# A gated DeltaNet layer: the inverse of the chunks' matrices by fp32 products on whole operands instead of three fp16 products on halves

## The chip, the cores and the metric

One Trainium2 chip, of which the program uses one core. The metric is the device time of one execution in microseconds (us). Several executions were timed, and one more was recorded by the hardware profiler.

## The reference, cut to what matters

One layer with two kinds of heads over a prompt of 4096 rows, and one step for 8 sample rows. The prompt's four DeltaNet heads are computed in chunks: inside a chunk a unit lower triangular matrix of 64x64 is solved, and only then the state of 128x128 is carried on.

```python
lower = eye + beta[..., :, None] * jnp.einsum('nbhtd,nbhid->nbhti', k, k) * dec_strict
rhs = jnp.concatenate([(beta * jnp.exp(G))[..., None] * k, beta[..., None] * v], -1)
sol = lax.linalg.triangular_solve(lower, rhs, left_side=True, lower=True, unit_diagonal=True)
...
def step(s, xs):
    u = ut_c - jnp.einsum('bhcd,bhde->bhce', w_c, s)
    o = jnp.einsum('bhcd,bhde->bhce', qd_c, s) + jnp.einsum('bhti,bhie->bhte', aqk_c, u)
    s = gl_c[..., None, None] * s + jnp.einsum('bhcd,bhce->bhde', kd_c, u)
```

Everything is fp32. After the heads come a gate, sliding-window attention with 8 heads of its own, an output product with the 1024x1024 matrix and a LayerNorm.

## The kernel before, in words

The program has two phases. Phase 1 (to about 1135 us) runs over 16 superblocks `s` of 256 prompt rows, each of two chunks `c` of 128 rows with four heads; phase 2 does the attention, the gate and the output product and is not touched.

For a superblock, `front` makes keys, queries and values: 12 blocks of 128 columns, each by 24 fp16 products of 128x256 into the PSUM tile `pj` (weights `w`, rows `hT`, both as high and low fp16 halves), then a short convolution on VectorE (L315) and a SiLU (L321, L322; tiles `kqv`, `vv`). The products of keys with keys and queries go to `pga` (L41) and VectorE scales them to `U`, which is minus the strict lower part of the matrix, and `Aqk` (L379, L382).

The inverse of I - U is made in three levels. `lanes` writes the 32x32 diagonal blocks of all heads to DRAM and reads them back so that each partition holds one column problem, solves them on VectorE in 31 dependent pairs of operations (L421, L423; tiles `lt`, `LV`, `LU`), and brings the results back by DMA as the block diagonal `VTd`. `gdn_inv` then joins 32x32 blocks to 64x64 and 64x64 to 128x128 by four products per head: `px`, `pv`, `p2`, `p3` (PSUM tile `pgi`). In the kernel before, each of these products is three fp16 products (`mm3` with `P3`: high by high, high by low, low by high); the halves are made by `sub`, a copy to fp16 on ScalarE (L452) and a subtraction on VectorE (L453). The halves of `U` and `VTd` are made once per superblock (L384, L385; L434, L435).

`gdn_c` uses the inverse `V` of a chunk in fp32 products with the state (`pgi<-S,kqv`, `pgi<-r,V`, `pgi<-ut,Kd`, `pgi<-ut,Aqk`), and `S` goes on to the next chunk.

Beside this, phase 1 prepares the next superblock's rows (`xt`: `x`, `hT`, L253 to L256), weights for phase 2 (`prep`, `prep_s`: `stg`, `stt`, `wt`, L529 to L573) and the sample rows (`gate_cols`, `dec_a`: `xt`).

The code's order is not that of the engines. A scheduler at build time gives each engine a fixed sequence from a cost model of its own, so that the projections `pj<-hT,w` of the next superblock and the solve of `lanes` are laced into the inverse and `gdn_c` of this one. At run time each engine follows its sequence and waits on semaphores. The figures below call two parts of a superblock's period by their first PE instruction: **part A** from the first `pgi<-S,kqv` (start of `gdn_c`) to the first `pga<-kqv` of the next superblock, and **part B** from there to the next `pgi<-S,kqv`; part B has the `pga` products and the inverse.

Of the kernel before, what the change touches and what calls it, by code (L numbers as in the profile page):

```python
# [33 lines left out]
def body(ctx, tc, I, O, seq):  # L34
# [5 lines left out]
    def mm(out, l, r, st=True, sp_=True):  # L40
        pe.matmul(out, l, r, start=st, stop=sp_)  # L41
# [69 lines left out]
    with ExitStack() as p1:  # L111
# [124 lines left out]
        XE = w1p.tile([128, 2, 4, 128], F16, name="XE")  # L236
        XZ = w1p.tile([128, 2, 4, 128], F16, name="XZ")
        V64 = w1p.tile([128, 2, 4, 64], F16, name="V64")
        VR = w1p.tile([128, 2, 4, 64], F16, name="VR")
        for t in (VTd, XE, XZ, V64, VR):  # L240
            pool.memset(t, 0.0)
# [18 lines left out]
        def front(s, hT, ahead):  # L260
# [26 lines left out]
            U = wk.tile([128, 8, 128], F32, name="U", bufs=1)  # L287
            U16 = wk.tile([128, 2, 8, 128], F16, name="U16", bufs=1)
# [94 lines left out]
            vt, vt16 = lanes(s, U)  # L383
            act.activation(U16[:, 0], U, AF.Copy)  # L384
            dve.tensor_sub(U16[:, 1], U, U16[:, 0])  # L385
# [17 lines left out]
            return kqv, G, sc, U16, Aqk, Kd, Vn, eGl, vt, vt16  # L403

        def lanes(s, U):

            d1, d2 = D1[s % 2], D2[s % 2]
            d1v = d1.rearrange("(m b) (i t) -> b i m t", b=4, t=32)
            for b in range(4):
                bs = slice(32 * b, 32 * b + 32)  # L410
                sp.dma_start(d1v[b], U[bs, :, bs])
            LU = w1p.tile([128, 32, 32], F32, name="LU", bufs=1)
            for c in range(4):
                sp.dma_start(LU[32 * c:32 * c + 32].rearrange("p a b -> p (a b)"), d1)
            LV = w1p.tile([128, 8, 32], F32, name="LV", bufs=1)
            dve.tensor_copy(LV.rearrange("p a b -> p (a b)"), lv0)
            lt = w1p.tile([128, 8, 32], F32, name="lt", bufs=1)
            for j in range(31, 0, -1):
                j0 = j // 4
                n = 8 - j0  # L420
                dve.tensor_mul(lt[:, j0:, 0:j], LV[:, j0:, j:j + 1].to_broadcast([128, n, j]),  # L421
                               LU[:, None, 0:j, j].to_broadcast([128, n, j]))
                dve.tensor_add(LV[:, j0:, 0:j], LV[:, j0:, 0:j], lt[:, j0:, 0:j])  # L423
            d2w = d2.rearrange("l (j c i) -> c l j i", c=4, i=32)
            for c in range(4):
                sp.dma_start(d2w[c], LV[32 * c:32 * c + 32])
            d2r = d2.rearrange("(m b) (q i) -> b q m i", b=4, i=32)
            vt = VTd
            for b in range(4):
                bs = slice(32 * b, 32 * b + 32)  # L430
                sp.dma_start(vt[bs, :, bs], d2r[b])
            vt16 = w1p.tile([128, 2, 8, 2, 32], F16, name="vt16")
            ve = vt.rearrange("p m (a b) -> p m a b", b=64)[:, :, :, 0:32]
            act.activation(vt16[:, 0], ve, AF.Copy)  # L434
            dve.tensor_sub(vt16[:, 1], ve, vt16[:, 0])  # L435
            return vt, vt16

        P3 = ((0, 0), (0, 1), (1, 0))

        def gdn_inv(c, U16, vt, vt16):  # L440

            V = wk.tile([128, 4, 128], F32, name="V", bufs=2)
            Vo = wk.tile([128, 2, 4, 2, 32], F16, name="Vo", bufs=1)
            xe, xz, v64, vr = XE, XZ, V64, VR
            m0 = 4 * c

            def mm3(out, l, r):
                for n, (a, b) in enumerate(P3):
                    mm(out, l(a), r(b), n == 0, n == 2)

            def sub(dst, src):
                act.activation(dst[0], src, AF.Copy)  # L452
                dve.tensor_sub(dst[1], src, dst[0])  # L453
# [5 lines left out]
            vo = V.rearrange("p h (a b) -> p h a b", b=64)[:, :, :, 32:64]  # L459
            sub([Vo[:, 0], Vo[:, 1]], vo)  # L460
            px = pgi.tile([128, 4, 2, 32], F32, name="pgi")
            for h in range(4):
                mm3(px[:, h], lambda a: U16[:, a, m0 + h, :], lambda b: vt16[:, b, m0 + h])
            sub([xe[:, z].rearrange("p h (a b) -> p h a b", b=64)[:, :, :, 0:32] for z in range(2)], px)
            pv = pgi.tile([128, 4, 2, 32], F32, name="pgi")
            for h in range(4):
                mm3(pv[:, h], lambda a: xe[:, a, h, :], lambda b: Vo[:, b, h])
            dve.tensor_copy(V[0:32, :, 32:64], pv[0:32, :, 0, :])
            dve.tensor_copy(V[64:96, :, 96:128], pv[64:96, :, 1, :])
            sub([vr[64:128, z] for z in range(2)], V[64:128, :, 64:128])  # L470
# [3 lines left out]
            sub([v64[0:64, z] for z in range(2)], pt[0:64, :, 0:64])  # L474
            p2 = pgi.tile([128, 4, 64], F32, name="pgi")
            for h in range(4):
                mm3(p2[:, h], lambda a: U16[:, a, m0 + h, :], lambda b: v64[:, b, h, :])
            sub([xz[64:128, z, :, 0:64] for z in range(2)], p2[64:128])
            p3 = pgi.tile([128, 4, 64], F32, name="pgi")
            for h in range(4):  # L480
                mm3(p3[:, h], lambda a: xz[:, a, h, :], lambda b: vr[:, b, h, :])
# [227 lines left out]
        def ahead(s):  # L709
            if s < NS:  # L710
                nxt[0] = xt(s, load_x(s))

        for s in range(NS):
            kqv, G, sc, U16, Aqk, Kd, Vn, eGl, vt, vt16 = front(s, nxt[0], lambda: ahead(s + 1))
            Vs = [gdn_inv(c, U16, vt, vt16) for c in range(2)]
# [741 lines left out]
```

## Time and profile before

| | us |
|---|---|
| median of 3 executions (2236.66 to 2239.43) | 2238.08 |
| the profiled execution | 2235.32 |
| its span, first to last instruction | 2233.5 |
| TensorE matmul busy (PE) | 2098.6 (94%) |
| VectorE busy (DVE) | 1831.9 (82%) |
| ScalarE busy (ACT) | 1269.1 (57%) |

Read it so: PE is the TensorE's matmul stream, PEld its weight loads, which run beside it; the granted clock is that of the TensorE as a share of 2.4 GHz, 0.982 over the span. Busy times are unions of the instructions' times; matmuls in a burst overlap, so the burst is much shorter than their number times the time of one.

### The profile page before, as it was taken

How to read it: one execution, taken by the hardware profiler on the slowest of the kernel's cores; microseconds unless marked ns; L12 is line 12 of the kernel's file. 1: busy time of each engine (PE TensorE's matmuls, PEld its weight loads, DVE VectorE, ACT ScalarE, POOL GpSimd, SP SyncE). 2: the span in 40 equal slices, each digit the busy share in tenths (PEclk: the TensorE clock that was granted, in tenths of full speed). 3: DMA queues.
4: the chain of work that ended last, by engine and by line, in shares of the span. 5: the costliest groups of instructions: out<-in, count | busy, mean ns of one | idle time of the engine just before them, and what ended most of it. 6: DMA issues, size and time to landing. Idle time of an engine off the chain costs nothing.

```text
span 2233.5 us, 48900 instructions
## 1 busy us (share of the span) xinstructions
PE 2098.6 (94%) x18287; PEld 1497.6 (67%) x18287; DVE 1831.9 (82%) x5546; ACT 1269.1 (57%) x3601; POOL 163.4 (7%) x284
## 2 busy tenths in 40 slices
PE   6989999999989999898999999999999999999997
PEld 4877888878778888777676777776445545444443
DVE  7778889888889989888878977776786787888877
ACT  6666877666767776655446666666443333334332
POOL 1101111111111111011000000000000000000000
PEclk9999999999999999999999999999998999999999
DMA  8333332332233332213153111110532333323222
GB/s 331 105 114 92 130 91 93 119 105 68 88 98 107 107 115 81 67 51 114 54 215 119 59 60 60 61 58 23 222 100 91 131 114 114 117 87 132 95 98 72
DMA packets 141679, 232.21 MB, mean 104 GB/s; under 512 B 62852, under 2 KB 75448, under 8 KB 135272
## 3 DMA queue, kind: packets, MB, share of 16 engines
q1 hardware_dynamic: 140144, 228.53, 30.1%
q8 instruction: 144, 2.36, 0.4%
q14 instruction: 95, 0.78, 0.1%
q10 hardware_dynamic: 1296, 0.55, 0.1%
HBM read 154.07 MB, written 76.09 MB: 103 GB/s over the span
## 4 chain that ended last, share of the span: by engine, by line
PE 53%; DVE 28%; ACT 11%; DMA 4%; issue 3%; POOL 0%; POOLq 0%; SPq 0%; ACTq 0%; DVEq 0%
PE pp L1042 21%; PE pj L41 11%; PE pgi L41 6%; DVE kqv L315 5%; DVE lt L421 3%; PE pga L41 3%; ACT Sm L872 3%; DVE LV L423 3%; PE po L41 2%; PE tr L41 2%; PE tr L889 2%; DMA x<-in_xT_dram 1%; DVE kqv L322 1%; PE xt L41 1%; PE pS L41 1%
## 5 line engine op out<-in xcount | busy, mean ns | idle before, releaser
L41 PE MATMUL pj<-hT,w 128*128 128x256 f16 x4608 | 575.7, 275 | 3.4 <-ACT hT L255 2.6
L41 PEld LDWEIGHTS <-w 128*128 128x128 f16 x4800 | 450.0, 99 | 65.1 <-issue 11.4
L1042 PEld LDWEIGHTS <-S 128*128 128x128 f16 x1536 | 150.6, 99 | 171.4 <-issue 5.0
L41 PEld LDWEIGHTS <-hT 128*128 128x128 f16 x2048 | 159.8, 98 | 68.8 <-issue 4.1
L41 PE MATMUL pj<-wq,hT 128*128 128x512 f16 x768 | 194.8, 379 | 1.1 <-DVE qt L783 0.6
L315 DVE SCALAR_TENSOR_TENSOR kqv<-u,cols,kqv 128x256 f32<-128x256 f32 x384 | 181.9, 480 | 3.7 <-ACT kqv L313 3.1
L1042 PE MATMUL pp<-wz,S 128*128 128x512 f16 x768 | 182.1, 383 | 0.0
L1042 PE MATMUL pp<-wo,S 128*128 128x512 f16 x768 | 171.3, 379 | 0.7 <-DVE zs L1218 0.6
L872 ACT ACTIVATE Sm<-Sm,nm 128x256 f32<-128x256 f32 (+1 forms) x256 | 125.5, 492 | 56.0 <-DVE nm L869 56.0
L1042 PE MATMUL pp<-wz,hT 128*128 128x512 f16 x576 | 131.9, 380 | 1.2 <-ACT zs L1129 1.2
L421 DVE TENSOR_TENSOR lt<-LV,LU 128x60 f32<-128x60 f32 (+24 forms) x496 | 120.2, 242 | 5.8
L1042 PE MATMUL pp<-wo,A 128*128 128x512 f16 x540 | 122.1, 379 | 0.0
L865 DVE CUSTOM_DVE_ANT_0 Sm<-pS,swam 128x256 f32<-128x256 f32 (+1 forms) x256 | 96.2, 415 | 28.2 <-PE tr L889 27.3
L423 DVE TENSOR_TENSOR LV<-LV,lt 128x60 f32<-128x60 f32 (+24 forms) x496 | 103.4, 208 | 5.8
L1042 PEld LDWEIGHTS <-hT 128*128 128x128 f16 x612 | 59.8, 98 | 71.8 <-issue 2.8
L41 PE MATMUL pj<-wkv,hT 128*128 128x256 f16 x768 | 105.6, 273 | 0.0
L1081 POOL TENSOR_TENSOR rs<-rs,cf 128x1 f32<-128x1 f32 (+1 forms) x33 | 22.8, 692 | 1070.7 <-DVE rs L1080 1070.7
L41 PE MATMUL pga<-kqv 128*128 128x256 f32 x256 | 72.2, 401 | 24.2 <-DVE kqv L322 24.1
L1042 PEld LDWEIGHTS <-A 128*128 128x128 f16 x540 | 52.8, 99 | 62.0
L1023 ACT ACTIVATE S<-zt 128x512 f16<-128x512 f32 x64 | 40.3, 630 | 85.7 <-DVE zt L1029 81.4
L1136 ACT ACTIVATE zs<-zs 128x512 f32<-128x512 f32 x48 | 30.2, 629 | 101.3 <-DVE zs L1135 101.2
L315 DVE SCALAR_TENSOR_TENSOR vv<-u,cols,vv 128x256 f32<-128x256 f32 x192 | 82.3, 479 | 1.7 <-ACT vv L313 1.0
(378 smaller groups left out, 4574.7 us busy)
## 6 DMA issues: line engine op xcount, KB each, us to landing
hT<-hD SPq DMA_DIRECT2D x32, 1024.0 KB
x<-in_xT_dram SPq DMA_DIRECT2D x32, 512.0 KB
hD<-hT SPq DMA_DIRECT2D x16, 1024.0 KB
x<-in_x_prompt_dram SPq DMA_DIRECT2D x60, 256.0 KB
out_y_prompt_dram<-x SPq DMA_DIRECT2D x60, 256.0 KB
stg<-in_ws_dram SPq DMA_DIRECT2D x16, 512.0 KB
LU<-D SPq DMA_DIRECT2D x64, 128.0 KB
wS<-wt SPq DMA_DIRECT2D x16, 512.0 KB
```

The source lines that it names most:

```text
L41: pe.matmul(out, l, r, start=st, stop=sp_)
L315: dve.scalar_tensor_tensor(d, u[:, b2, j:j + 256], cwj(j, blk), d, op0=ALU.mult, op1=ALU.add)
L322: dve.scalar_tensor_tensor(dst, th, 1.0, dst, op0=ALU.add, op1=ALU.mult)
L421: dve.tensor_mul(lt[:, j0:, 0:j], LV[:, j0:, j:j + 1].to_broadcast([128, n, j]), LU[:, None, 0:j, j].to_broadcast([128, n, j]))
L423: dve.tensor_add(LV[:, j0:, 0:j], LV[:, j0:, 0:j], lt[:, j0:, 0:j])
L865: dve.tensor_tensor_reduce(Sm[:, h, k0:256], pS[:, h2, k0:256], swam[:, k0:256], 0.125, -1e30, op0=ALU.add, op1=ALU.max, accum_out=mx[:, h ...
L872: act.activation(Sm[:, h, k0:256], Sm[:, h, k0:256], AF.Exp, bias=nm[:, h:h + 1], accum_out=sm_[:, h:h + 1])
L889: pe.transpose(pt[:, h2, kb, :], Sm[:, h + h2, kb * 128:(kb + 1) * 128], ident)
L1023: act.activation(q[:, 0], src, AF.Copy)
L1042: pe.matmul(dst.rearrange("p (u c) -> p u c", c=128), A[:, hi, k, :], W[:, k // 2::2, q, wi, k % 2, :], start=new and n == 0, stop=n == 11 ...
L1081: pool.tensor_tensor(rs[0:n, 1:2], rs[0:n, 0:1], half_neg[0:n, 0:1], op=ALU.pow)
L1136: act.activation(zs, zs, AF.Silu, scale=IWS)
```

## The change

The four products take whole fp32 operands: one fp32 product per head and level in place of three fp16 products. The halves, the tiles for them and the operations that make them are gone; `U` gets a second buffer, since the products now read it directly; `VTd` and `V` are read in place. DMAs and all other products stay as many as they were.

```diff
-        XE = w1p.tile([128, 2, 4, 128], F16, name="XE")
-        XZ = w1p.tile([128, 2, 4, 128], F16, name="XZ")
-        V64 = w1p.tile([128, 2, 4, 64], F16, name="V64")
-        VR = w1p.tile([128, 2, 4, 64], F16, name="VR")
+        XE = w1p.tile([128, 4, 128], F32, name="XE")
+        XZ = w1p.tile([128, 4, 128], F32, name="XZ")
+        V64 = w1p.tile([64, 4, 64], F32, name="V64")
...
-            U = wk.tile([128, 8, 128], F32, name="U", bufs=1)
-            U16 = wk.tile([128, 2, 8, 128], F16, name="U16", bufs=1)
+            U = wk.tile([128, 8, 128], F32, name="U", bufs=2)
...
-            vt, vt16 = lanes(s, U)
-            act.activation(U16[:, 0], U, AF.Copy)
-            dve.tensor_sub(U16[:, 1], U, U16[:, 0])
+            vt = lanes(s, U)
...
-            vt16 = w1p.tile([128, 2, 8, 2, 32], F16, name="vt16")
-            ve = vt.rearrange("p m (a b) -> p m a b", b=64)[:, :, :, 0:32]
-            act.activation(vt16[:, 0], ve, AF.Copy)
-            dve.tensor_sub(vt16[:, 1], ve, vt16[:, 0])
-            return vt, vt16
+            return vt
...
-            def mm3(out, l, r):
-                for n, (a, b) in enumerate(P3):
-                    mm(out, l(a), r(b), n == 0, n == 2)
-
-            def sub(dst, src):
-                act.activation(dst[0], src, AF.Copy)
-                dve.tensor_sub(dst[1], src, dst[0])
...
-            vo = V.rearrange("p h (a b) -> p h a b", b=64)[:, :, :, 32:64]
-            sub([Vo[:, 0], Vo[:, 1]], vo)
+            ve, vo = quarters(vt[:, m0:m0 + 4])[:, :, :, 0:32], quarters(V)[:, :, :, 32:64]
             px = pgi.tile([128, 4, 2, 32], F32, name="pgi")
             for h in range(4):
-                mm3(px[:, h], lambda a: U16[:, a, m0 + h, :], lambda b: vt16[:, b, m0 + h])
-            sub([xe[:, z].rearrange("p h (a b) -> p h a b", b=64)[:, :, :, 0:32] for z in range(2)], px)
+                mm(px[:, h], U[:, m0 + h, :], ve[:, h])
+            act.activation(quarters(XE)[:, :, :, 0:32], px, AF.Copy)
             pv = pgi.tile([128, 4, 2, 32], F32, name="pgi")
             for h in range(4):
-                mm3(pv[:, h], lambda a: xe[:, a, h, :], lambda b: Vo[:, b, h])
+                mm(pv[:, h], XE[:, h, :], vo[:, h])
             dve.tensor_copy(V[0:32, :, 32:64], pv[0:32, :, 0, :])
             dve.tensor_copy(V[64:96, :, 96:128], pv[64:96, :, 1, :])
-            sub([vr[64:128, z] for z in range(2)], V[64:128, :, 64:128])
...
-            sub([v64[0:64, z] for z in range(2)], pt[0:64, :, 0:64])
+            act.activation(V64, pt[0:64, :, 0:64], AF.Copy)
             p2 = pgi.tile([128, 4, 64], F32, name="pgi")
             for h in range(4):
-                mm3(p2[:, h], lambda a: U16[:, a, m0 + h, :], lambda b: v64[:, b, h, :])
-            sub([xz[64:128, z, :, 0:64] for z in range(2)], p2[64:128])
+                mm(p2[:, h], U[0:64, m0 + h, :], V64[:, h, :])
+            act.activation(XZ[64:128, :, 0:64], p2[64:128], AF.Copy)
             p3 = pgi.tile([128, 4, 64], F32, name="pgi")
             for h in range(4):
-                mm3(p3[:, h], lambda a: xz[:, a, h, :], lambda b: vr[:, b, h, :])
+                mm(p3[:, h], XZ[64:128, h, :], V[64:128, h, 64:128])
```

The scheduler then orders all engines anew. On TensorE, in the inverse of superblock 8 in the middle of phase 1, a piece around the second product (`pgi<-Vo,XE`) stands so before; `w_5_360` is a projection's weight, and each fp16 product has a weight load (LDWEIGHTS) of its own in the list:

```order
L41 LDWEIGHTS w_5_360
L41 MATMUL pj<-hT,w_5_360 128x256
L41 LDWEIGHTS XE
L41 MATMUL pgi<-Vo,XE 128x64
L41 LDWEIGHTS w_5_360
L41 MATMUL pj<-hT,w_5_360 128x256
```

The same place in the change; an fp32 product is one row here, its weight loads not being listed apart, and x4 are the four heads:

```order
L440 MATMUL pgi<-cf,VTd 128x128 x4
L41 MATMUL pgi<-VTd,U 128x64 x4
L41 MATMUL pga<-kqv 128x256
L41 LDWEIGHTS w_10_398
L41 MATMUL pj<-hT,w_10_398 128x256
L41 MATMUL pgi<-V,XE 128x64 x4
```

What moved: the inverse now begins among the `pga` products of the next superblock, and fewer projections stand in it. Over superblocks 1 to 12 the sequence before has on average 197 projections in part A and 89 in part B; in the change they are 236 and 50.

On VectorE, the inverse of superblock 8 before, from the low half of `vt` on:

```order
L435 TENSOR_TENSOR vt_9323<-VTd,vt_9323 128x512
L315 SCALAR_TENSOR_TENSOR vv<-u,cols,vv 128x256 x4
L453 TENSOR_TENSOR Vo<-V,Vo 128x256
L453 TENSOR_TENSOR XE<-pgi,XE 128x8x32
L668 TENSOR_TENSOR dt_10702<-xt,deg 128x4
L256 TENSOR_TENSOR hT<-x,hT 128x512
L468 COPY V<-pgi 32x4x32
L469 COPY V<-pgi 32x4x32
L322 SCALAR_TENSOR_TENSOR vv<-th,vv 128x1024
```

And in the change, from the first chunk's inverse (the copies to `V`, L450 and L451) through the second's, and on into `gdn_c` (`r`, `ut`):

```order
L450 COPY V<-pgi 32x4x32
L451 COPY V<-pgi 32x4x32
L380 TENSOR_TENSOR Aqk<-pga,dec 128x256
L649 TENSOR_TENSOR dt_9839<-xt,deg 128x4
L650 SCALAR_TENSOR_TENSOR ddl<-dy,dt_9839 128x4
L651 TENSOR_TENSOR ddl<-ddl,dbe 128x4
L652 TENSOR_TENSOR dt_9839<-xt,deg 128x4
L653 TENSOR_TENSOR doT<-ddl,dqk 128x4
L654 TENSOR_TENSOR doT<-doT,dt_9839 128x4
L313 SCALAR_TENSOR_TENSOR vv<-u,cols,vv 128x256 x2
L474 SCALAR_TENSOR_TENSOR r<-pgi,G,Vn 128x128 x4
L313 SCALAR_TENSOR_TENSOR vv<-u,cols,vv 128x256 x2
```

What moved: of the subtractions nothing is left, and work that stood among them (the last convolutions and the SiLU of `vv`, the low halves of `hT`, the preparation of phase 2's weights) now stands behind `r`, that is in part A.

## Rows read from the trace of the kernel before

**Rows 1.** The page: busy time of the engines, the span in 40 slices.

```profile
PE 2098.6 (94%) x18287; PEld 1497.6 (67%) x18287; DVE 1831.9 (82%) x5546; ACT 1269.1 (57%) x3601; POOL 163.4 (7%) x284
PE   6989999999989999898999999999999999999997
PEclk9999999999999999999999999999998999999999
```

**Rows 2.** Windows: superblock 0, superblocks 1 to 13, superblock 14; bounds at `pgi<-cf,VTd`.

```profile
core 0: us, PE busy (x) PEld busy (x) DVE busy (x) ACT busy (x) POOL busy (x), PEclk, DMA share, GB/s
158.50:220.70 62.20, 54.02 (x474) 46.68 (x472) 52.35 (x170) 37.71 (x121) 9.60 (x12) 0.90 0.31 99
220.70:1047.50 826.80, 772.90 (x7753) 668.73 (x7752) 728.47 (x2546) 566.85 (x1833) 108.90 (x194) 0.99 0.30 95
1047.50:1102.20 54.70, 45.90 (x382) 33.82 (x381) 45.96 (x168) 26.69 (x81) 1.20 (x2) 0.91 0.27 83
```

**Rows 3.** Waits of PE, 220.7 to 1047.5 us: total, times, longest.

```profile
PE pga L41 <- DVE kqv L322: 19.7, 13, 2.1
PE tr L41 <- DVE g L283: 8.2, 7, 2.8
PE pgi L41 <- ACT V L452: 3.3, 7, 1.8
...
PE tr L355 <- DVE kqv L322: 3.2, 4, 1.0
```

**Rows 4.** Windows over part A of superblocks 1 to 12: one, and the sum.

```profile
684.81:722.27 37.46, 34.87 (x324) 30.81 (x325) 36.49 (x139) 27.45 (x91) 7.16 (x11) 1.00 0.30 100
...
sum 462.90, PE 427.14 PEld 382.05 DVE 436.46 ACT 325.81 POOL 88.25; mean PE 35.59 PEld 31.84 DVE 36.37 ACT 27.15 POOL 7.35
```

**Rows 5.** Windows over part B of the same superblocks: one, and the sum.

```profile
722.27:749.18 26.91, 25.95 (x290) 21.76 (x290) 23.42 (x73) 18.74 (x56) 0.82 (x4) 1.00 0.33 93
...
sum 297.90, PE 283.70 PEld 233.89 DVE 239.84 ACT 200.07 POOL 13.89; mean PE 23.64 PEld 19.49 DVE 19.99 ACT 16.67 POOL 1.16
```

**Rows 6.** Timeline of PE and PEld: start, length, shape and number of a burst.

```profile
678.73 0.51 PE L41 MATMUL pgi<-vt,U 128*128 128x64 f16 x12
691.05 1.06 PE L41 MATMUL pgi<-ut,Aqk 128*128 128x128 f32 x8
699.45 4.86 PE L41 MATMUL pj<-hT,w 128*128 128x256 f16 x43
729.80 0.95 PE L41 MATMUL xt<-dkq,stg 128*128 128x2 f32 x8
729.69 0.97 PEld L41 LDWEIGHTS xt<-dkq,stg 128*128 128x128 f32 x8
```

**Rows 7.** Instruction groups with mean times, PE and PEld, all of phase 1.

```profile
L41 PE MATMUL pgi<-vt,U x384: 189/193/261, 159.4 to 1110.9; 128*128 128x64 f16 x192
L41 PE MATMUL pgi<-ut,Aqk x256: 275/275/275, 180.4 to 1129.7; 128*128 128x128 f32 x128
L41 PEld LDWEIGHTS pgi<-ut,Aqk x256: 192/192/192, 180.3 to 1129.6; 128*128 128x128 f32 x128
```

**Rows 8.** Groups on VectorE by form, 220.7 to 1047.5 us: busy, mean ns, idle before.

```profile
L322 DVE SCALAR_TENSOR_TENSOR vv<-th,vv 128x1024 f32<-128x1024 f32 x13 | 15.9, 1221 | 0.9 <-ACT th L321 0.7
L385 DVE TENSOR_TENSOR U<-U,U 128x1024 f16<-128x1024 f32 x13 | 15.9, 1220 | 1.3 <-ACT U L384 1.3
L453 DVE TENSOR_TENSOR XZ<-pgi,XZ 64x256 f16<-64x256 f32 x26 | 11.1, 428 | 4.6 <-ACT XZ L452 3.9
L453 DVE TENSOR_TENSOR Vo<-V,Vo 128x256 f16<-128x256 f32 x26 | 11.0, 422 | 5.6 <-ACT Vo L452 5.4
L256 DVE TENSOR_TENSOR hT<-x,hT 128x512 f16<-128x512 f32 x48 | 32.4, 683 | 0.1
L435 DVE TENSOR_TENSOR vt<-VTd,vt 128x512 f16<-128x512 f32 x13 | 9.0, 689 | 3.4 <-ACT vt L434 3.4
L559 DVE TENSOR_TENSOR wt<-stg,wt 128x1024 f16<-128x1024 f32 x12 | 14.6, 1221 | 0.0
```

**Rows 9.** The same on ScalarE.

```profile
L384 ACT ACTIVATE U<-U 128x1024 f16<-128x1024 f32 x13 | 13.7, 1057 | 0.3
L452 ACT ACTIVATE Vo<-V 128x256 f16<-128x256 f32 x26 | 10.7, 412 | 0.3
```

More of the change, by code (lines that the diff above doesn't have):

```diff
@@ L235, in body @@
         VTd = w1p.tile([128, 8, 128], F32, name="VTd")
-        XE = w1p.tile([128, 2, 4, 128], F16, name="XE")
-        XZ = w1p.tile([128, 2, 4, 128], F16, name="XZ")
-        V64 = w1p.tile([128, 2, 4, 64], F16, name="V64")
-        VR = w1p.tile([128, 2, 4, 64], F16, name="VR")
-        for t in (VTd, XE, XZ, V64, VR):
+        XE = w1p.tile([128, 4, 128], F32, name="XE")
+        XZ = w1p.tile([128, 4, 128], F32, name="XZ")
+        V64 = w1p.tile([64, 4, 64], F32, name="V64")
+        for t in (VTd, XE, XZ):
             pool.memset(t, 0.0)
@@ L402, in front @@
                     act.activation(Vn[:, m, :], pv[:, h, :], AF.Copy, scale=sc[:, 0, m:m + 1])
-            return kqv, G, sc, U16, Aqk, Kd, Vn, eGl, vt, vt16
+            return kqv, G, sc, U, Aqk, Kd, Vn, eGl, vt
         def lanes(s, U):
@@ L431, in lanes, with gdn_inv, quarters @@
                 sp.dma_start(vt[bs, :, bs], d2r[b])
-            vt16 = w1p.tile([128, 2, 8, 2, 32], F16, name="vt16")
-            ve = vt.rearrange("p m (a b) -> p m a b", b=64)[:, :, :, 0:32]
-            act.activation(vt16[:, 0], ve, AF.Copy)
-            dve.tensor_sub(vt16[:, 1], ve, vt16[:, 0])
-            return vt, vt16
-        P3 = ((0, 0), (0, 1), (1, 0))
-        def gdn_inv(c, U16, vt, vt16):
+            return vt
+        def gdn_inv(c, U, vt):
             V = wk.tile([128, 4, 128], F32, name="V", bufs=2)
-            Vo = wk.tile([128, 2, 4, 2, 32], F16, name="Vo", bufs=1)
-            xe, xz, v64, vr = XE, XZ, V64, VR
             m0 = 4 * c
-            def mm3(out, l, r):
-                for n, (a, b) in enumerate(P3):
-                    mm(out, l(a), r(b), n == 0, n == 2)
-            def sub(dst, src):
-                act.activation(dst[0], src, AF.Copy)
-                dve.tensor_sub(dst[1], src, dst[0])
+            def quarters(t):
+                return t.rearrange("p h (a b) -> p h a b", b=64)
             pb = pgi.tile([128, 4, 128], F32, name="pgi")
@@ L713, in body @@
         for s in range(NS):
-            kqv, G, sc, U16, Aqk, Kd, Vn, eGl, vt, vt16 = front(s, nxt[0], lambda: ahead(s + 1))
-            Vs = [gdn_inv(c, U16, vt, vt16) for c in range(2)]
+            kqv, G, sc, U, Aqk, Kd, Vn, eGl, vt = front(s, nxt[0], lambda: ahead(s + 1))
+            Vs = [gdn_inv(c, U, vt) for c in range(2)]
             for c in range(2):
```

## The prediction

> **What bounds the kernel now.** I read the page first: TensorE (PE) is busy 94% of the span and VectorE (DVE) 82%, and the slices show PE near full from one end to the other, the granted clock being 0.99 in the middle of phase 1 [rows 1, 2]. So nothing on PE is free unless it falls into one of PE's few idle spots. Then I cut phase 1 into windows. In superblocks 1 to 13 PE is busy 772.9 of 826.8 us, so 53.9 us are idle, 4.1 per superblock of 63.6; superblocks 0 and 14 have 8.2 and 8.8 us idle each, since there are no projections to lace in at either end [rows 2]. The list of PE's waits says whom the idle time belongs to: 31.1 of the 53.9 us are waits for VectorE, before the `pga` products (19.7), for the decay `g` (8.2) and before the transposes of the keys (3.2); the largest wait on ScalarE is 3.3 [rows 3].
>
> VectorE is not late everywhere. Cut into the two parts, superblocks 1 to 12 take 38.6 us in part A (462.9/12) with PE busy 35.6 and DVE 36.4, and 24.8 us in part B (297.9/12) with PE 23.6 and DVE 20.0 [rows 4, 5]. Part A is thus VectorE's: 94% busy, it ends when VectorE gives up the last `kqv`, and PE waits there. Part B, with the inverse, is PE's: 95% busy, while DVE stands at 81% and itself waits for ScalarE's halves [rows 5, 8]. Over both, PE and DVE hand the bound to each other once per superblock.
>
> **The change, part by part.**
>
> *Products on PE.* A group (one product for four heads) is now twelve fp16 matmuls of 64 columns. Such a burst lasts 0.51 us with 0.193 for one, so a matmul costs (0.51-0.193)/11 = 0.029, a group 0.35 us [rows 6, 7]. An fp32 product appears in the trace as two matmuls with two weight loads: the `gdn_c` products are 32 chunks of four, and 256 of each are counted [rows 7]. With 128 columns a pass costs (1.06-0.275)/7 = 0.112. No fp32 product of 64 columns with 128 columns of weights is there, so its price is bounded. From above: with only 2 columns the eight weight loads of four products still take 0.97 us, (0.97-0.192)/7 = 0.111 each [rows 6]; narrower columns buy nothing, the weight load paces it. Eight of these are 0.89 us. From below: if only columns counted and fp32 were four times a 64-column matmul, sixteen by 0.029, 0.46 us. I take 0.89, because 64 columns lie between the 2 and the 128 that cost the same. So a group costs 0.54 us more; eight groups per superblock 4.3, all sixteen 69 us, superblocks 1 to 13 alone 56.
>
> The Trainium skill ("FP8 and Floating Point Precision", TensorE Precision Notes) says that true fp32 is four passes through the array. By that rule alone, four against three, a group would cost 0.12 more and the whole kernel some 15 us of PE, an estimate from that page. The rows disagree as far as narrow operands go: two records per product, each held at 0.111 by its weights.
>
> 56 us more on 772.9 are 829 us, more than the 826.8 that these superblocks now take. Even if PE never waited again, the middle of phase 1 would be 2 us longer. This is the main argument: VectorE's relief can only fill PE's idle time, which the products have already used up.
>
> *Work taken from VectorE and ScalarE.* Per superblock: the low halves of `U` (1.22 us) and `VTd` (0.69), and ten subtractions of about 0.42 (five for each chunk; two of the five rows stand for all): 6.1 us of DVE busy time, and about 1.2 us of waits for ScalarE in front of those that are shown ((1.3+4.6+5.6+3.4)/13) [rows 8]. ScalarE loses the copies of `U` (1.06), `VTd` and, twice, of `Vo` and `VR` (0.41 each) [rows 9]; it is 57% busy, and I cost that at nothing. Were all in VectorE's part, it would be worth its whole time. But only `U`'s low half lies in part A, by the order in five of twelve superblocks; the rest lies in part B, where PE is the bound.
>
> *The chain of a chunk's inverse.* Before, a product waits for the high half, then PE does one matmul and the low half (0.42) comes behind it. Now there is one copy and then 0.89 us. Four times (0.42 + 0.35) against four times 0.89: nearly even, so in superblock 0, where nothing covers the chain, I cost the change at nothing.
>
> *What the new order moves.* Projections in part A rise from 197 to 236 per superblock and fall from 89 to 50 in part B. A projection costs 4.86/43 = 0.11 us [rows 6], so 4.3 us of PE go from B to A. Six fp32 transposes of `vv` (0.11 each) and eighteen small products of the decay (0.03 each, the smallest spacing shown) go with them: 1.1. Behind `r`, thus in part A, VectorE now has 2.6 more low halves of `hT` (0.68 each, 1.8), the SiLU of `vv` and one convolution more (1.22+0.48), some 2.3 us of the preparation for phase 2 (most of it `wt` at 1.22), less 0.5 for `U`: together +5.3 (durations from [rows 8], numbers of instructions counted in the two orders).
>
> *Sum.* Part A: PE 35.6+4.3+1.1 = 41.0, with 0.5 for ScalarE's waits 41.5; DVE 36.4+5.3 = 41.7, with the 2.2 us for which it stands idle there now 43.9. The two engines are almost level, so I take a value between, 42.8, or 4.2 more than now. Part B: PE 23.6-4.3-1.1+4.3 = 22.5, and with its present 1.2 of waits 23.7, 1.1 less. Together +3.1 per superblock, 40 us for thirteen. At the ends: superblock 0 nothing; superblock 14 has in the new order 27 projections in its inverse where it had none, against 8.8 us idle, for which I give back 4; superblock 15 lies under phase 2's work on a full PE and pays most of its 4.3, say 3. That is +39 on the profiled execution's 2235.3, or **2274 us**. The median of the runs is 2238.1, 0.1% above that execution; I leave this as it is.
>
> What is late next: in part A VectorE again, now with more to do and less of PE's idle time to hide it; in part B the copies on ScalarE between two groups.
>
> **The rivals.**
>
> *The weight loads hide (the other side).* If a group cost its columns only, 0.46, part B would be 23.7-3.4 = 20.3, and the new order, which has moved 5.4 us of PE into part A, would be repaid: 41.5 to 42.8 + 20.3 = 61.8 to 63.1 against 63.4, thus 2210 to 2230. It decides at about 0.5 us per group. For it speaks that weight loads run beside matmuls; against it that four products of two columns, between projections, take their full 0.95 us [rows 6]. The page on four passes, named above, would lead here.
>
> *PE alone is the bound.* If VectorE's relief removes its waits outright, part A is 41.5 and part B, without the waits for low halves, 23.0: 64.5, +1.1 per superblock, 2250. For it: DVE loses 6.1 us of 56 (728.47/13) [rows 2]. Against it: it gains 5.3 of work in the very part where it was late.
>
> *VectorE sets part A and part B gains nothing.* 43.9 + 24.8 = 68.7, +5.3, 2304. For it: fewer projections lie between two dependent groups, so PE may stand while ScalarE copies (0.4 us each, eight per superblock). Against: four to eight projections or a `pga` product are still put into nearly every such place.
>
> **How the numbers follow.** Forecast, 2260 to 2292: 0.53. PE alone, 2244 to 2260: 0.20. VectorE in part A and waits in B, above 2292: 0.16. Weight loads hide: 0.11, of which I give 0.07 to faster and 0.04 to the same. What this kernel's measurement can tell from no change is about 0.2%, 4.5 us. Faster 0.07, same 0.05 (with 0.01 from the lower edge of PE alone), slower 0.88. The range reaches from PE alone to the third rival's value: 2249 to 2303.
>
> **What the profile after would show.** Right: 64 fp32 records in place of 96 fp16 ones per superblock for the four products; bursts of eight at about 0.111 us a pass; the rows L452 and L453 for halves gone; PE busy up by 65 to 70 us, DVE down by some 85 to 95; superblocks 1 to 13 some 40 us longer, part A about 43 us with DVE still near 95%, part B about a microsecond shorter, phase 2 as it was. Wrong in the price, if the bursts of 64 columns show 0.06 or 0.2 a pass. Wrong in the order, if the waits of PE for `kqv` and `g` are gone (then 2250) or if long waits for ScalarE appear before `pgi<-V,XE`, `pgi<-V,U` or `pgi<-V,XZ` (then 2300).

## The result, and the profile after

The change takes 2310.93 us (median of 4 executions, 2309.41 to 2316.99) against 2238.76 for the kernel before beside it: ratio 1.0335, 95% interval 1.0318 to 1.0352. It is slower, as forecast, but by 72 us and not by 36: 2310.9 lies above 2274 and above the range's upper end of 2303. One execution of e5 below (2480.36 us) ran at a granted clock of 0.83 and is left out of the comparisons.

The page of the profiled execution (2309.41 us, span 2307.6), the lines of [rows 1]:

```profile
PE 2174.7 (94%) x17775; PEld 1580.8 (69%) x17775; DVE 1743.9 (76%) x5354; ACT 1218.8 (53%) x3505; POOL 172.0 (7%) x282
PE   6989999999999999999898999999999999999997
PEclk9988999999999999999999999999999999999999
```

TensorE (PE) has 76 us more and 512 records less (32 for each superblock), VectorE (DVE) 88 us less. PE's share is 94% as before: its idle time has hardly shrunk (132.9 us, was 134.9). In the clock, slices 3 and 4 (115 to 231 us, superblock 0) have become an 8. Over the span the clock is 0.975, was 0.982: what is missing to full clock is some 58 us against 40, an estimate from these shares of the two spans. So up to 18 of the 76 us are a slower clock and not more work.

The windows of [rows 2], bounds again at `pgi<-cf,VTd`:

```profile
157.89:227.79 69.90, 62.45 (x444) 55.26 (x442) 46.95 (x159) 34.89 (x115) 9.72 (x12) 0.83 0.27 89
227.79:1105.31 877.52, 827.07 (x7292) 731.24 (x7291) 654.96 (x2380) 525.61 (x1748) 118.06 (x194) 0.98 0.28 88
1105.31:1169.21 63.90, 57.86 (x440) 43.94 (x438) 46.13 (x177) 27.41 (x89) 2.21 (x3) 1.00 0.30 97
```

The span grew by 74.1 us: superblock 0 by 7.7 (forecast 0), superblocks 1 to 13 by 50.7 (forecast 40), superblock 14 by 9.2 (forecast -4), and the rest by 7.1 (forecast 3; 2307.6 - 1169.2 against 2233.5 - 1102.2); the start is 0.6 shorter. In superblocks 1 to 13 PE is busy 54.2 us more and idle 50.4 us, was 53.9.

PE's timeline in the inverse of superblock 8, against [rows 6]:

```profile
704.29 1.00 PE L41 MATMUL pgi<-VTd,U 128*128 128x64 f32 x8
705.77 1.10 PE L41 MATMUL pgi<-V,XE 128*128 128x64 f32 x8
709.20 1.10 PE L41 MATMUL pgi<-V,U 64*128 64x64 f32 x8
710.77 1.10 PE L41 MATMUL pgi<-V,XZ 64*128 64x64 f32 x8
```

Eight passes a group, from 1.00 to 1.10 us with the last one's own 0.27 to 0.30 in it: some 0.11 a pass, and with that the 0.89 of the forecast.

PE's waits in superblocks 1 to 13, against [rows 3]:

```profile
PE pga L41 <- DVE kqv L320: 19.8, 13, 2.2
PE tr L41 <- DVE g L282: 12.1, 9, 2.6
PE tr L353 <- ACT G L332: 3.8, 3, 1.9
```

VectorE has a tenth less to do there (655 us, was 728), and PE waits for `kqv` as long as before (19.7) and for `g` longer (8.2). Long waits for ScalarE's copies before `pgi<-V,XE`, `pgi<-V,U` or `pgi<-V,XZ` have not come up.

Part A and then part B of superblocks 1 to 12, the sums, against [rows 4, 5]:

```profile
sum 540.76, PE 498.92 PEld 450.93 DVE 485.77 ACT 377.69 POOL 103.86; mean PE 41.58 PEld 37.58 DVE 40.48 ACT 31.47 POOL 8.65
...
sum 275.31, PE 270.06 PEld 228.80 DVE 124.84 ACT 111.82 POOL 7.50; mean PE 22.50 PEld 19.07 DVE 10.40 ACT 9.32 POOL 0.63
```

Part A takes 45.1 us (forecast 42.8), part B 22.9 (23.7): 68.0 for a superblock, 4.6 more than before and 0.3 more than the price of the products alone. (What lies outside these twelve superblocks in the middle is 4.6 us shorter than before, so that the thirteen grew by 50.7.) VectorE's relief is real, but it shows as idle time of VectorE in part B (10.4 busy of 22.9).

The clock differs in these windows too: eleven of the 24 show 0.93 to 0.96 in the change, three before. One of part A and one of part B:

```profile
584.03:633.01 48.98, 45.27 (x424) 41.22 (x424) 42.92 (x163) 35.04 (x112) 8.67 (x13) 0.95 0.41 135
351.80:377.67 25.87, 25.77 (x192) 22.27 (x192) 11.96 (x36) 11.26 (x33) 0.57 (x3) 0.93 0.21 52
```

Length times what is missing to 1.00, added up, gives some 19 us in the change and 5 before, an estimate: about 14 of the 54 us that PE is busy longer. What makes the clock fall in these places is not shown.

### The profile page after: what moved, and what is told of

Its sections match the earlier page's. It is cut to its first block, busy times and chain, and to the rows that moved or that the text cites. A ratio compares the mean times of both kernels' runs of the same rounds, so it can differ in the third digit from the quotient of the medians.

```text
span 2307.6 us, 47590 instructions
## 1 busy us (share of the span) xinstructions
PE 2174.7 (94%) x17775; PEld 1580.8 (69%) x17775; DVE 1743.9 (76%) x5354; ACT 1218.8 (53%) x3505; POOL 172.0 (7%) x282
## 4 chain that ended last, share of the span: by engine, by line
PE 47%; DVE 14%; ACT 6%; issue 2%; DMA 2%; POOL 0%; POOLq 0%; SPq 0%; ACTq 0%; DVEq 0%
PE pp L1023 20%; PE pj L41 10%; PE pgi L41 6%; DVE kqv L313 2%; ACT Sm L853 2%; PE po L41 2%; PE tr L870 2%; DVE lt L417 1%; PE pga L41 1%; PE pS L41 1%; PE tr L41 1%; DVE LV L419 1%; DMA dw<-in_wdec_dram 1%; DVE bst L1058 1%; DVE x L1066 1%
## 5 line engine op out<-in xcount | busy, mean ns | idle before, releaser
L41 PE MATMUL pj<-hT,w 128*128 128x256 f16 x4608 | 566.8, 275 | 3.2 <-ACT hT L254 2.6
L41 PEld LDWEIGHTS <-w 128*128 128x128 f16 x4800 | 456.6, 99 | 58.1 <-issue 3.6
L853 ACT ACTIVATE Sm<-Sm,nm 128x256 f32<-128x256 f32 (+1 forms) x256 | 125.5, 492 | 88.7 <-DVE nm L850 88.6
L377 DVE SCALAR_TENSOR_TENSOR U<-pga,sc,dec 128x128 f32<-128x128 f32 x128 | 39.1, 345 | 66.2 <-PE pga L41 65.9
```

The costliest lines, as they stand in the source:

```text
L377: dve.scalar_tensor_tensor(U[:, m, :], pa[:, h2, 1, :], sc[:, 3, m:m + 1], decs[c][:, 2 * hp + h2, :], op0=ALU.mult, op1=ALU.mult)
L853: act.activation(Sm[:, h, k0:256], Sm[:, h, k0:256], AF.Exp, bias=nm[:, h:h + 1], accum_out=sm_[:, h:h + 1])
```

## The experiments

*Theory 1*: the time follows TensorE's own work, and VectorE's relief is worth nothing. Rivals: *theory 2*, the new order lengthens part A; *theory 3*, the relief is worth something and a larger price hides it. Times are medians; the ratios are to the kernel before in the same series.

**The relief alone, and the price alone.** Two kernels made from the one before. In the first (e1):

```diff
-            dve.tensor_sub(U16[:, 1], U, U16[:, 0])
-            dve.tensor_sub(vt16[:, 1], ve, vt16[:, 0])
-                dve.tensor_sub(dst[1], src, dst[0])
-                for n, (a, b) in enumerate(P3):
-                    mm(out, l(a), r(b), n == 0, n == 2)
+                for _ in P3:
+                    mm(out, l(0), r(0))
```

> The kernel before without any of the subtractions that make the low halves (U, VTd and the ten of a superblock), TensorE's work unchanged: each of the four products issues three fp16 matmuls on the high halves, of which the last stands (so the products are fp16 products of the high halves alone). VectorE loses its 88 us, TensorE gains nothing. Its order at build time already is that of the change: 233 projections in part A and 51 in part B per superblock (before 197 and 89, change 236 and 50). Theory 1 (time is TensorE's, the relief is worth nothing): 2234 to 2242, waits for kqv and g as before. Theory 2 (the new order, by itself, lengthens part A, because VectorE's work piles up behind r): 2245 to 2265, part A 41 to 43 us. Theory 3 (the relief is worth VectorE's waits, but the change hides it under a larger price on TensorE): 2205 to 2225, waits for kqv and g well under 20 us.

Measured: 2230.17, ratio 0.9971 (0.9957 to 0.9984), 6 us. Superblocks 1 to 13:

```profile
218.53:1026.38 807.85, 753.99 (x7701) 666.00 (x7700) 655.41 (x2380) 561.57 (x1822) 104.97 (x194) 0.99 0.30 95
1026.38:1088.42 62.04, 54.17 (x477) 39.84 (x476) 46.05 (x178) 31.31 (x100) 2.32 (x3) 1.00 0.31 105
```

The second row is superblock 14. The middle is 19 us shorter, but superblock 14 is 7.3 longer and the rest behind it 4.4: with the new order, work that stood in the middle comes later. That answers theory 2 too: this order, with 233 projections in part A, costs nothing as a whole. In all, 88 us of VectorE are worth 6, and not by filled waits: PE is idle 53.9 us in the middle as before (807.85 - 753.99), and over the span 142.0, was 134.9. What fell is its busy time, with as many records (18287) in another order. Theory 3 falls, theory 1 was off by the 6.

In the second (e2), VectorE keeps its work and PE gets more:

```diff
+                for _ in range(4 + h % 2):
+                    mm(out, l(0), r(0))
                 for n, (a, b) in enumerate(P3):
```

> The kernel before with all halves, and 18 more fp16 matmuls of 64 columns in each group (four or five more per head, overwritten by the three that count), so that a group takes 30 times 0.029 = 0.87 us, the price of the fp32 group, while VectorE keeps its subtractions. Its order has 236 projections in part A and 51 in part B. Theory 1: before plus 128 times 0.52 = 67 us, that is 2300 to 2310, hardly less than the change. Theory 2: the same order with more work on VectorE, so part A is longer than in the change: 2320 to 2340. Theory 3: the relief is missing, so that the time is the change plus what the relief is worth, 2325 or more.

Measured: 2308.67, ratio 1.0322 (1.0294 to 1.0350), +72 for 67 us of matmuls. That is the change's time without fp32 and without the relief, though not by the same terms: in e2's profiled execution the clock is 0.987 (0.975 in the change), PE is busy 57 us longer than before and idle 9 longer.

**The change with the halves still made (e3):**

```diff
+            U16 = wk.tile([128, 2, 8, 128], F16, name="U16", bufs=1)
+            act.activation(U16[:, 0], U, AF.Copy)
+            dve.tensor_sub(U16[:, 1], U, U16[:, 0])
...
+            sub([quarters(XE2[:, z])[:, :, :, 0:32] for z in range(2)], px)
             pv = pgi.tile([128, 4, 2, 32], F32, name="pgi")
```

> The change with all the high and low halves of before still made (copies on ScalarE, subtractions on VectorE), into tiles that nobody reads; the products stay fp32. 215 projections in part A and 69 in part B, between the two orders. Theory 1: as the change, 2306 to 2316. Theory 2 (VectorE's chain sets part A): 2320 to 2345, with longer waits for kqv. Theory 3: 2325 to 2340.

Measured: 2304.72, ratio 1.0312 (1.0275 to 1.0348), not slower than the change. Superblocks 1 to 13:

```profile
229.59:1106.43 876.84, 829.28 (x7334) 734.37 (x7333) 736.09 (x2546) 590.17 (x1911) 104.98 (x194) 0.98 0.29 89
```

81 us more on VectorE than in the change, in the same 877 us. PE waits for `kqv` 20.5 us there (19.8 in the change) and for `g` 16.7 (12.1), but it is idle 47.6 in all (50.4). "VectorE sets part A" falls with it.

**Half of the weight columns (e4):**

```diff
-                mm(p2[:, h], U[0:64, m0 + h, :], V64[:, h, :])
+                mm(p2[64:128, h], U[0:64, m0 + h, 64:128], V64[:, h, :])
-                mm(p3[:, h], XZ[64:128, h, :], V[64:128, h, 64:128])
+                mm(p3[0:64, h], XZ[64:128, h, 0:64], V[64:128, h, 64:128])
```

> The change with only the needed half of the weights in the last two products: p2 takes columns 64 to 128 of U, p3 columns 0 to 64 of XZ, 64 weight columns instead of 128 (the other half of each product is never read, or zero). The order is that of the change (236 and 49). If a pass is paced by the number of weight columns, these groups take about 0.45 instead of 0.89 us, 64 groups, 28 us less on TensorE: Theory 1: 2280 to 2288. Theory 2 (part A is VectorE's and the saving lies in part B): also about 2283, since the inverse lies in part B. If a pass has a fixed price whatever the weights' columns: 2308 to 2316.

Measured: 2276.30, ratio 1.0178 (1.0155 to 1.0202), 35 us less than the change. The timeline of the weight loads (PEld) in superblock 7, a group with whole weights and two with half. The last row is from the change, superblock 8, where such a group still has whole weights:

```profile
688.32 0.97 PEld L41 LDWEIGHTS pgi<-V,XE 128*128 128x128 f32 x8 [0.27 <-ACT XE L446]
691.75 0.54 PEld L41 LDWEIGHTS pgi<-V,U 64*64 64x64 f32 x8 [0.33 <-issue]
692.90 0.54 PEld L41 LDWEIGHTS pgi<-V,XZ 64*64 64x64 f32 x8 [0.21 <-ACT XZ L459]
...
709.20 0.96 PEld L41 LDWEIGHTS pgi<-V,U 64*128 64x128 f32 x8 [0.33 <-issue]
```

With the same 64 moving columns and on the same 64 partitions, a group falls from 0.96 to 0.54 us when its weight columns are halved: the weight load paces an fp32 pass. 64 such groups are 27 us at full clock; superblock 0 alone fell from 69.9 to 65.9. The few us that are left I have not separated; the clock is 0.979 here, 0.975 in the change.

**The chain ahead of `pga`.** Why did the waits for `kqv` stay? DVE, ACT and PE in the change, ahead of one first `pga` product:

```profile
763.79 2.47 DVE L313 SCALAR_TENSOR_TENSOR kqv<-u,cols,kqv 128x256 f32<-128x256 f32 x6 [0.29 <-ACT kqv L311]
766.29 1.06 ACT L319 ACTIVATE th<-kqv 128x1024 f32<-128x1024 f32 x1 [2.24 <-DVE kqv L313]
767.38 1.23 DVE L320 SCALAR_TENSOR_TENSOR kqv<-th,kqv 128x1024 f32<-128x1024 f32 x1 [1.12 <-ACT th L319]
768.66 1.13 PE L41 MATMUL pga<-kqv 128*128 128x256 f32 x4 [0.73 <-DVE kqv L320]
```

From the last convolution's end, tanh and SiLU take the 2.4 us up to `pga`, here as in the kernel before (2.40 to 2.66 in its superblocks 1 to 13). The convolutions ahead of them wait for ScalarE's copies of PE's own projections (`[0.29 <-ACT kqv L311]`). Work taken from VectorE elsewhere does not shorten that. *Theory 1b*: PE's idle time there is this chain. The split (e5 and e9, made from the change):

```diff
+                    if grp == 0:
+                        half = slice(2 * pr, 2 * pr + 2)
+                        th = wf.tile([128, 4, 256], F32, name="th", bufs=1)
+                        act.activation(th[:, half], dst[:, half], AF.Tanh, scale=0.5)
+                        dve.scalar_tensor_tensor(dst[:, half], th[:, half], 1.0, dst[:, half], op0=ALU.add, op1=ALU.mult)
                     if pr == 0:
                         yield
+                if grp == 0:
+                    return
```

> The change, with the SiLU of the queries (tanh on ScalarE, product on VectorE) made in two halves of two heads, each behind its own three-tap convolutions, instead of one behind all: the same arithmetic, only the last chain before pga is shorter. In every superblock of all kernels run so far the last 4.87 us before pga are six convolutions (2.47), tanh (1.06) and SiLU (1.22) without a gap, and PE stands 1.5 us per superblock at their end. Theory 1b (PE's idle time is this chain's length, not VectorE's load): the chain is 1.1 us shorter and the first pga product needs the first half only, so the waits for kqv fall from 19.8 to under 8 us and the time by 10 to 16 us, to 2295 to 2301. Theory of load (PE waits because VectorE has too much to do in part A): no work is taken away, 2306 to 2316.

> The change with the split SiLU of the queries once more, since its profiled execution ran at a granted clock of 0.83 and its stages can't be compared. Time 2280 to 2290 as then, 26 us below the change. Theory 1b (the chain ahead of pga): superblocks 1 to 13 take about 850 us (877.5 in the change), the waits for kqv are under 8 us. Theory of the clock (the split only happened to keep superblock 0 at full clock, as the filling did): superblock 0 takes 57 us instead of 69.9 and superblocks 1 to 13 at least 865.

Measured: 2282.72 to 2284.56, ratio 1.0213 (1.0191 to 1.0236), and again 2284.01, ratio 1.0208 (1.0186 to 1.0229): 27 us less than the change, twice what was expected. Windows of superblocks 0 and 1 to 13:

```profile
154.30:226.40 72.10, 63.72 (x448) 56.27 (x446) 47.52 (x162) 34.92 (x116) 10.76 (x12) 0.81 0.26 86
226.40:1077.20 850.80, 811.88 (x7293) 720.43 (x7292) 656.80 (x2392) 531.92 (x1766) 105.04 (x194) 0.99 0.29 90
```

The longest of PE's waits in the latter:

```profile
PE tr L41 <- DVE g L282: 7.9, 8, 1.9
PE tr L360 <- ACT Kd L364: 6.5, 12, 0.9
PE tr L360 <- ACT G L339: 5.2, 4, 1.9
PE tr L392 <- DVE kqv L320: 4.2, 9, 0.8
```

The gain lies in the middle, not in superblock 0's clock; of the waits of `pga` for `kqv` not one is left, with no work taken from VectorE. But only part of it is idle time: in the middle PE is idle 38.9 us, 11.5 less than in the change, which is what theory 1b expected, and busy 15.2 less with as many records (7293, 7292), at a clock of 0.99 for 0.98. Whether that second part comes from the split is not shown: over the span the clock was 0.979 to 0.985 in e9's executions and 0.973 to 0.978 in the change's. The same split in the kernel before (e6):

> The same split of the queries' SiLU in the kernel before (175 projections in part A and 111 in part B). Theory 1b: 10 to 16 us less than before, 2220 to 2227, thus below both kernels, the waits for kqv falling from 19.7 to under 8. Theory of load: VectorE is 94% busy in part A here, no work is taken away, 2234 to 2241.

Measured: 2228.62, ratio 0.9969 (0.9954 to 0.9984), 7 to 9 us: faster than the kernel before and the change, the wait before `pga` gone here too, but new ones for `kqv` at the transposes (8.2 and 5.2) and for `r` (6.5) take most of its place. PE's idle time in the middle falls by 5.0 (819.5 - 770.6 = 48.9), its busy time by 2.3.

**Does VectorE's load count once the chain is short (*theory 2b*)?** The split in e1 (e13) and in e3 (e14), no other edit:

> The kernel before without the subtractions (as in the run without them, each product issuing three fp16 matmuls on the high halves alone) and with the split SiLU of the queries. Theory 2b (VectorE's load counts only once the chain ahead of pga is short): 10 to 20 us below the split alone (2228.6), 2209 to 2219. Theory of the sum (the relief is worth its 6 us whatever the chain): 2220 to 2225.

Measured: 2222.47, ratio 0.9943 (0.9929 to 0.9956), 6 below e6, with PE idle 136.8 us over the span, more than in e6 (129.3).

> The change with the halves of before still made for nobody, and with the split SiLU. Theory 2b: the load of 88 us on VectorE that cost nothing ahead of the split now costs 12 to 20 us against the split alone (2284), 2296 to 2305. Theory of the sum: 2278 to 2286.

Measured: 2292.41, ratio 1.0259 (1.0243 to 1.0275), 8 to 11 above e9: between the two expectations, with PE idle 126.6 us over the span (125.5 in e9) and a clock of 0.978 for 0.984. The times alone would make the load worth 6 to 11 us with the split and 0 to 6 without it, but PE's idle time shows no such price. Theory 2b falls at the size that I gave it. The split brings 27 us in the change and 7 to 9 in the kernel before; more than half of the 27 is busy time of PE, at a higher clock, and of idle time in the middle it is 11.5 against 5.0.

A third of the load on GpSimd instead, in e6 (e15):

```diff
-            dve.tensor_sub(U16[:, 1], U, U16[:, 0])
+            pool.tensor_sub(U16[:, 1], U, U16[:, 0])
-            sub([vr[64:128, z] for z in range(2)], V[64:128, :, 64:128])
+            act.activation(vr[64:128, 0], V[64:128, :, 64:128], AF.Copy)
+            pool.tensor_sub(vr[64:128, 1], V[64:128, :, 64:128], vr[64:128, 0])
```

> The kernel before with the split SiLU and with two of the subtractions (the low halves of U, and VR's of both chunks) on GpSimd, which is busy 7%, instead of VectorE: 1.2 + 2 times 0.42 = 2 us per superblock, 33 of the 88, full precision kept. Theory 2b: 3 to 7 us below the split alone, 2221 to 2226. Theory of the sum: 2 us, 2225 to 2229. If GpSimd takes so long over a low half that the products wait for it: above 2232.

Measured: 2236.46, ratio 1.0008 (0.9999 to 1.0017): the split's gain is lost. `U`'s low half takes 2.37 us on GpSimd (1.22 on VectorE). And VectorE is hardly relieved: 48 subtractions, 33 us, have left it, but over the span it is busy 1824.4 us (1829.1 in e6). Some of its own operations take longer, above all the first of the solve, in e6 and then in e15:

```profile
L428 DVE TENSOR_TENSOR lt<-LV,LU 128x31 f32<-128x31 f32 x13 | 2.7, 207 | 0.2
L428 DVE TENSOR_TENSOR lt<-LV,LU 128x31 f32<-128x31 f32 x13 | 10.1, 776 | 0.0
```

In the timeline of e15, one of these operations, else 0.2 us, lasts as long as the subtraction on GpSimd beside it:

```profile
357.63 2.13 POOL L392 TENSOR_TENSOR U<-U,U 128x1024 f16<-128x1024 f32 x1 [2.51 <-ACT U L391]
357.81 2.02 DVE L428 TENSOR_TENSOR lt<-LV,LU 128x30 f32<-128x30 f32 x1
```

Which wait of PE costs the gain I have not shown.

**Superblock 0's clock.** The windows from the first inverse on, in the change (columns as above, the granted clock third from the end):

```profile
157.89:163.89 6.00, 4.13 (x30) 3.52 (x27) 1.26 (x3) 2.45 (x5) 0.00 (x0) 0.82 0.12 46
163.89:169.89 6.00, 5.44 (x26) 5.16 (x25) 1.52 (x4) 1.72 (x4) 0.00 (x0) 0.50 0.63 221
169.89:175.89 6.00, 4.11 (x17) 3.36 (x17) 2.16 (x10) 0.76 (x2) 0.00 (x0) 0.50 0.00 0
175.89:181.89 6.00, 5.47 (x25) 5.17 (x25) 0.00 (x0) 1.70 (x3) 0.00 (x0) 0.50 0.00 1
```

After a stretch in which PE stood still in one place after another the granted clock is 0.50, that is 1.2 instead of 2.4 GHz, for some 20 us, and a group of fp32 products takes 1.96 us there:

```profile
175.42 1.96 PE L41 MATMUL pgi<-V,U 64*128 64x64 f32 x8 [0.53 <-ACT V L455]
177.91 1.96 PE L41 MATMUL pgi<-V,XZ 64*128 64x64 f32 x8 [0.53 <-ACT XZ L459]
```

The Trainium skill ("TensorE: Matmul & The Clock Gate", "The HAM clock gate") has these two levels and says that activity releases the higher one. These rows show both levels, and in e7, where PE is kept busy, the higher one stays. The filling (e7), behind each of the five copies of a chunk:

```diff
+            def fill():
+                if s == 0:
+                    pz = pgi.tile([128, 2, 256], F32, name="pgi")
+                    for n in range(8):
+                        mm(pz[:, n % 2], id16, c16)
```

> The change, with eight fp16 products of 128x256 behind each of the five copies of a chunk's inverse in superblock 0 only, into a PSUM tile that nobody reads: 80 products, 8.8 us of work at 0.11, in the places where PE waits for a copy. In the change the granted clock is 0.50 from 164 to 182 us, in the middle of superblock 0's inverse, and superblock 0 takes 69.9 us. Theory of the clock (superblock 0's extra 7.7 us are the low clock, which follows PE's idle places): with the places filled the clock stays at 0.9 or more, superblock 0 takes 60 to 65 us and the time is 4 to 9 us less than the change, 2302 to 2307. Theory of the chain (its fp32 groups and copies are simply longer): superblock 0 takes 70 to 79 us, the time is 2311 to 2320.

Measured: 2296.62, ratio 1.0269 (1.0245 to 1.0292), 14 us less than the change, with 80 products more; I had expected 4 to 9. Superblock 0, and two of its windows:

```profile
154.90:211.00 56.10, 52.95 (x464) 47.26 (x462) 42.69 (x143) 30.57 (x99) 6.85 (x11) 1.00 0.31 102
...
160.90:166.90 6.00, 6.00 (x53) 5.24 (x51) 1.95 (x10) 1.65 (x5) 0.00 (x0) 1.00 0.26 82
166.90:172.90 6.00, 6.00 (x53) 5.06 (x50) 4.19 (x14) 1.79 (x4) 0.00 (x0) 1.00 0.27 99
```

The order moved as well: superblock 0 has 384 products without the fillers (444 in the change), the middle 58 more, in 876.8 us as before. The clock over the span is 0.985, was 0.975; how much of the 14 us is the order's is not separated.

**Less work on PE (e8)**, from e1:

```diff
-                for _ in P3:
-                    mm(out, l(0), r(0))
+                mm(out, l(0), r(0))
```

> The kernel before with the high halves alone (no low halves made) and one fp16 product per head and level in place of three: a group is four matmuls, 0.12 us instead of 0.35, 128 groups, 30 us less on TensorE than in the run with the high halves issued three times (2230). Theory 1 (the time follows TensorE's own work one for one in this direction too): 2197 to 2205. Theory of load (VectorE and the chains hold the middle of phase 1 by now): 2212 to 2232.

Measured: 2207.28, ratio 0.9873 (0.9850 to 0.9895), 22 to 23 below e1 for 30 us of matmuls: three quarters, between the two theories.

**All that helped, together.** Split and fillers in the kernel before (e10), and split, fillers and narrow weights in the change (e11):

> The kernel before (fp16 halves) with the split SiLU and with the fillers in superblock 0's inverse (80 fp16 products of 128x256 that nobody reads). The two are worth 9 us apart from the clock and, superblock 0 going from 64 us at a clock of 0.85 to about 56, another 6 to 8: 2220 to 2224 if they add up, 2228 if the filling buys nothing here.

Measured: 2233.28, ratio 0.9990 (0.9979 to 1.0001), 5 us more than the split alone. Superblock 0 takes 64.4 us (64.2 in e6), the clock falling to 0.62 a little later, behind the fillers. The loss itself lies further on: the middle is 6.5 shorter, but superblock 14 is 3.8 longer and what follows it 6.2.

> The change with all that helped it: split SiLU (26 us), fillers in superblock 0 (14), 64 weight columns in the last two products (35): 2236 if the three add up, which would be the time of the kernel before; 2245 to 2260 if the split and the fillers' gains are the same microseconds (superblock 0).

Measured: 2249.80, ratio 1.0051 (1.0036 to 1.0067). Of the 76 us that the three brought one by one, 61 remain, and the kernel before stays ahead.

**The second buffer of `U` (e12):**

```diff
-            U = wk.tile([128, 8, 128], F32, name="U", bufs=2)
+            U = wk.tile([128, 8, 128], F32, name="U", bufs=1)
```

> The change with one buffer for U instead of two, the part of the change that is no arithmetic. The products read U itself, so that pga of the next superblock has to wait until this one's inverse has read it; in the order all 288 projections of a superblock now stand between pga and the next state product, none in part A. Theory 1 (only TensorE's work counts): 2306 to 2320. Theory of the second buffer (it lets the solve on VectorE run beside the next superblock's products): well above, 2400 or more, VectorE's solve lying bare.

Measured: 2623.86, ratio 1.1724 (1.1704 to 1.1744). PE's longest waits over the span:

```profile
PE tr L395 <- DVE vv L320: 25.0, 15, 7.3
PE pga L41 <- DVE kqv L320: 22.7, 16, 2.3
PE pgi L454 <- DVE V L451: 22.3, 27, 0.8
PE pgi L440 <- DMA VTd<-D: 21.1, 8, 4.4
```

Without it superblocks 1 to 13 take 1151 us: the solve's DMAs and links of the inverse stand bare. Of the 311 us that the profiled span is longer, 147 are PE's idle time; it is also busy 164 longer, with the same 17775 records, at a granted clock of 0.902 (0.975).

## Why the prediction was right, and where it failed

*The price* of a group was right. 0.89 us for a group was taken from eight weight loads of two-column products; the bursts show it, and e4 shows the reason, since half of the weight columns take 0.54 instead of 0.97. The rival "the weight loads hide" falls. The four passes of the Trainium skill ("FP8 and Floating Point Precision", TensorE Precision Notes) gave an estimate of 15 us for the whole kernel, four passes against three. The bursts do not bear that out.

*The step that failed is "VectorE's relief can only fill PE's idle time"*, as the sum then used it. The products cost 4.3 us per superblock, and I charged 3.1 in superblocks 1 to 13 and gave 4 back in superblock 14: 36 us for the fourteen, where the price is 14 x 4.3 = 60. Measured: 50.7 + 9.2 = 59.9. In the terms of the sum: PE's idle time in part A was to shrink from 3.0 to 1.8 us per superblock, because the two engines were "almost level", while part B kept its 1.2. It came to 3.5 and 0.4, 3.9 together, where 4.2 stood before and 3.0 were forecast. The relief gave next to nothing back. e1 puts it at 6 us without any price, none of it from PE's idle time, and e3 at nothing beside the price.

That 59.9 meets the 60 so closely is luck. PE is busy 54.2 us longer in the middle (56 said), but some 14 of these are the clock, for which the sum had no term; the work itself came out nearer to 40. There 461 records are gone, 416 of them by the products themselves, the other 45 to superblock 14 for the most part, and e1 shows that another order alone can lower PE's busy time. I have not taken this apart further.

Behind the failed step stands a misreading of [rows 3, 4]: that PE waits for VectorE and VectorE is 94% busy, and that part A therefore ends by VectorE's amount of work. A wait for an engine need not be a wait for its load. The wait for `kqv` is the end of a chain of convolutions, tanh and SiLU whose last 2.4 us are the same in both kernels. Shortening the chain took the wait away (e9); adding 81 us to VectorE did not lengthen the time (e3).

*Part A and part B* were bounded apart (42.8 between 41.5 and 43.9; it came to 45.1). That failed too: e3 has about 20 projections fewer in part A than the change and the same 877 us. Only the sum means something, since the order moves work freely between them.

*Superblock 0 "nothing"* failed mostly by its clock. I compared the two chains at full speed, and in [rows 2] its clock was already 0.90; in the change it is 0.83. At 0.50 a group costs twice as much. With the places filled (e7) superblock 0 takes 56.1 instead of 69.9 us.

*Superblock 14, "for which I give back 4"*, has the wrong sign, and is the largest single miss: 13 of the 35 us by which the profiled span missed the sum. The new order brings it 27 projections. They filled little: PE's idle time went from 8.8 to 6.0, its busy time up by 12.0. The superblock grew by 9.2, and by 7.3 already in e1, where the products cost nothing more. In e3, which has no projections there, it takes 63.4 us all the same, at a clock of 0.81 (1.00 in the change), so that the cause is open. This has to be read with the middle, which e1's order makes 19 shorter.

*Forecasts of the profile*: PE up by 76 (65 to 70 said), DVE down by 88 (85 to 95), DVE in part A 90% busy (near 95). Of the rivals, "VectorE sets part A and part B gains nothing", 2304, came nearest in time, and its 68.7 us per superblock are nearly the 68.0 measured. Its mechanism is refuted by e3. "PE alone" needed the waits for `kqv` and `g` to go; they stayed.

With 69 us as the price in all sixteen superblocks, the 74.1 of the span leave 5: superblock 0 has 3.4 above its own 4.3, what lies ahead of it and behind superblock 14 has 2.2 (7.1 - 0.6 - 4.3), the fourteen between -0.3.

This sum counts the clock's share as price. Open: what lowers the clock in the middle of the change, and how much of the single gains is the order that each kernel got, since it differs in most of them.

## What to carry to other kernels

Charge work that is added to the busiest engine in full, and credit relief of another engine only where a row shows that the wait ends by that engine's amount of work, not by a chain of fixed length: look at the last few microseconds before the wait, link by link. Price an fp32 product by its weight columns, and cut those that nobody reads. When a product is to read a tile directly instead of a copy, ask how long the tile is held then: here its second buffer is worth 313 us. And before a difference is shared out among causes, compare the granted clock of the two profiles: here it is worth up to 18 of 74 us.

## What the hardware showed that I had not expected

- An fp32 pass with 64 moving columns is paced by its weight columns: (0.97 - 0.191)/7 = 0.111 us with 128 of them, (0.54 - 0.134)/7 = 0.058 with 64 (e4; the means of one load are in these rows).

```profile
L41 PEld LDWEIGHTS pgi<-V,XE 128*128 128x128 f32 x208 | 25.8, 191 | 4.7 <-ACT XE L446 3.8
L41 PEld LDWEIGHTS pgi<-V,U 64*64 64x64 f32 x208 | 14.0, 134 | 7.5 <-ACT V L455 4.4 <-issue 3.0
```

- A kernel with 80 products more that nobody reads was 14 us faster: in superblock 0's inverse the granted clock stayed at 1.00 where it had been 0.50. In another order (e10) the fall only came later.
- The clock added to the waits in e12: PE is idle 147 us longer there, and at a clock of 0.902 it is also busy 164 us longer with the same number of products.
- Subtractions on GpSimd hardly relieved VectorE (e15): 33 us were moved, 4.7 came off, and an operation of VectorE went from 0.21 to 0.78 us in the mean.
